# A two-layer GLA and SSD backbone in one program: one chunk's exponentials issued at another place, and a background computation paused over a layer norm

## The chip, the cores and the metric

The kernel runs on one core of a Trainium2 chip. The metric is the time of one execution on the device in microseconds (us); the time before is the median of three runs, 1932.36 us (1931.04 to 1933.9).

## What is computed

Two layers work on a stream of 512 latent tokens and 256 context tokens, 1024 channels each, all in float32. Layer 0 mixes tokens with gated linear attention (GLA, four heads), layer 1 with a bidirectional Mamba-2 state-space scan (SSD, eight groups of four heads of 64 channels, state of 128). Each mixer is followed by a squared-ReLU MLP of width 4096. Every sub-layer's input is modulated by a shift and a scale that come from the conditioning vectors, and its output by a gate; the sum with the residual goes through a layer norm.

```python
for i in range(DEPTH):                       # DEPTH = 2, kind 0 is GLA, kind 1 is SSD
    m_l = jnp.split((s_lat @ ada_w[i] + ada_b[i])[:, None, :], 6, axis=-1)
    ...
    hl = layer_norm(DEEPNORM_ALPHA * hl + m_l[2] * snake(yl), ln_g[i, 0], ln_b[i, 0])
    hl = layer_norm(DEEPNORM_ALPHA * hl + m_l[5] * sq_relu_mlp(modulate(hl, m_l[3], m_l[4]), ffn_w1[i], ffn_w2[i]), ...)

# SSD, one chunk of one direction; cum is the running sum of dt * a
seg = cum[:, :, None] - cum[:, None, :]
decay = jnp.exp(jnp.where(mask, seg, -jnp.inf))
cb = jnp.einsum('bign,bjgn->bijg', ci, bi)
y = jnp.einsum('bijg,bijgr,bjgrp->bigrp', cb, decay, xdt)
y = y + jnp.einsum('bign,bigr,bgrpn->bigrp', ci, jnp.exp(cum), s)
s_new = s * jnp.exp(last)[..., None, None] + jnp.einsum('bjgn,bjgr,bjgrp->bgrpn', bi, jnp.exp(last[:, None] - cum), xdt)
```

## The kernel before

**Products.** Channels lie on the 128 partitions and tokens along the free axis. Every weight matrix is read in blocks of 1024 x 128. A block is loaded by SP (`wload`, L258) and split in two parts that TensorE takes as fp32r: ScalarE (ACT) casts it to `wh` (L224) and VectorE (DVE) subtracts to get the rest `wl` (L225). `prod` (L265 to L273) then multiplies three times per block of 128 input channels: xh by wh, xl by wh, xh by wl, all at L271. These products, with 768, 512 or 384 token columns, are most of TensorE's (PE's) work.

**How side work is slotted in.** Each matmul in `prod` reports its columns to `worked` (L200 to L209). Every 768 columns are one unit. A list `side` holds Python generators with the inner work of the previous head or group, or with a layer norm; a generator that yields n is taken up again n units later. A second list, `background`, is advanced once in every `pace[0]` units, whenever the unit counter `clock[1]` is a multiple of it. `drain` runs the side generators to their end. So the place of inner work in the program is set by its yields, in units of matmul work. The framework's scheduler then orders the instructions of each engine by when it reckons their operands ready and by their place in the program; `tc.issue_after(ins)` keeps an instruction behind another one that it doesn't depend on.

**Background rows.** `ada_rows` (L154 to L182) computes the modulation vectors of later sub-layers on DVE: for each of eight blocks a load and one or two dot products over 1024 elements (L178), one block per step, each kept behind the last evacuation of the MLP (`behind`, L122). During the first MLP its items are the last rows of layer 0 and all of layer 1; the generator is appended at the end of the program's layer 0, where `pace[0]` is set to 21 (L1275).

**The first MLP's start.** `ffn` (L394) begins when the layer norm ahead of it is still under way. For the first two blocks of W1 it first multiplies the segments that are normalized (`presegs`, context and the first 256 latent tokens), then drains the layer norm, whose evacuation (L384 on ACT, L225 on DVE) brings the last 256 tokens, and then multiplies those (`restsegs`). After that `pace[0]` is 19, and from the second half of the first batch on 22.

**An SSD group.** `group(g)` (L938) projects and convolves the channels of group g: B, C, two blocks of x (`conv`: product, copy to `pre` on ACT at L914, five taps at L921 and L923, tanh form of SiLU at L925 and L926), then two gates. Then it appends `inner(g)`, which runs beside the products of group g + 1. Its steps, with the yields between them:

- At the start: eight row loads `ec` (L961) of cumulated decays, and for chunks 0 and 1 two tiles L each (L966), loaded by a broadcast row `crowc` (L968) and masked on GpSimd (POOL, L970). Ten L tiles exist.
- Transposition of B and x to natural layout (`natural`, L935, L936): `Bn`, `xnat`. Yields 1, 7, 7.
- States: products by decay weights (`prep`, `scaled_by`, L993), state contributions (`dS`, L1005), and the chain over chunks (`chain`, L993 and L1013). Yield 5, then the scores `cb` (L1025) and their copy `cbs` (L1027), yield 1, more of the chain, yield 2, the rest of it.
- For each half i of the head channels (`inter`): yield 4, an exponential of ec, four matmuls L1048 with the states, DVE products L1049, POOL sum L1050, DVE sum L1051 with the skip term.
- `decays` for a chunk: eight exponentials (L1060) over 128 x 128 on ACT, four for each direction, with the bias of their column. `ahead(c)` issues them behind the ACT instruction that `evac[0]` names, the last evacuation at that point. `ahead(0)` stands after `inter(0)`.
- For chunk c, every 14 units: `masks`, a POOL sum of both directions (L1063) and the DVE product with the scores (L1064), which is the mask tile; `ahead(c + 1)`; the rows of chunk c + 2; and in the next round `outputs` (four matmuls L1071 with xnat, two of 64 rows each side by side, and a DVE sum).

The functions that the change touches:

Of the kernel before, what the change touches and what calls it, by code (L numbers as in the profile page):

```python
# [12 lines left out]
AF = mybir.ActivationFunctionType  # L13
# [26 lines left out]
ZB = 2  # L40
# [23 lines left out]
def tile_backbone(ctx, tc, xT, cc, cr, vecs, rows, ada_w0, ada_wr, lnf, ffn_w1, ffn_w2,  # L64
                  gla_w_in, gla_w_v, gla_w_a, gla_a2, gla_w_out, ssd_w_in, ssd_w_dt, ssd_w_out, out):
    nc = tc.nc
# [18 lines left out]
    def nm(s):  # L85
        cnt[0] += 1
        return f"{s}_{cnt[0]}"
# [103 lines left out]
    clock = [0, 0]  # L191
# [19 lines left out]
    wait, pace = [0], [9]  # L211

    def drain(keep=0):
        while len(side) > keep:
            advance(side)
# [178 lines left out]
    def ffn(layer, xs, acc, segs, pool, npre, presegs, restsegs, passes, after):  # L394
# [29 lines left out]
        for bi, nb in enumerate((8, 8, 8, 8 - nlast, nlast)):  # L424
            ms = range(h0, h0 + nb)
            if bi == 0:
                drain(1)
                held = []
                for m in ms[:npre]:
                    held.append((weights(W1, m), mm_ps(segs)))  # L430
                    prod(held[-1][1], held[-1][0], xs, presegs, KT)
                drain()
                for m in ms[:npre]:
                    f1(m, restsegs, held[m])
                pace[0] = 19
                ms = ms[npre:]
            if bi == 4:
                ws = pair_weights(W2, h0, nb,
                                  lambda j: [pool.tile([P, NN], F32R, tag="rs", name=nm("ws"), bufs=20) for _ in range(2)])
            for m in ms:  # L440
                f1(m, segs if m == DFF // P - 1 else whole)
            ys = [rs[m] for m in range(h0, h0 + nb)]
            if bi == 0:
                gate = mod(layer, 5)
                pace[0] = 22
            if bi < 4:
                accum_proj(W2, h0, nb, ys, gate, acc, whole)
            else:
                accum_last(ws, ys, gate, acc, passes, after, early=None if layer == 0 else 5)
            h0 += nb  # L450
# [335 lines left out]
    def ssd_layer(xs, accd, acc0):  # L786
# [169 lines left out]
        def inner(g, fB, fC, fx, zs):  # L956
# [66 lines left out]
            for c in range(NLC):  # L1023
                cs = slice(c * P, (c + 1) * P)
                nc.tensor.matmul(cb[:, c, :], fB[:, cs], fC[:, cs], start=True, stop=True)  # L1025
            cbs = sp.tile([P, NLC, P], F32, tag="cbs", name=nm("cbs"), bufs=1)
            nc.scalar.copy(cbs, cb)  # L1027
            yield 1
            d03 = dS(*x03)
            chain(ST[1][:, 0], ST[0][:, 0], 0, 0, d03[:, 0])  # L1030
            chain(ST[2][:, 1], ST[3][:, 1], 3, 1, d03[:, 1])
# [18 lines left out]
                nc.gpsimd.tensor_add(T[:, i], T[:, i], E)  # L1050
                nc.vector.scalar_tensor_tensor(T[:, i], fx[i][:, 0:NL], dcol[:, 2 * g + i:2 * g + i + 1], T[:, i], ALU.mult, ALU.add)  # L1051

            def decays(c, L):
                for z, t in enumerate(L):
                    if z >= ZB:
                        nc.scalar.activation(t, t, AF.Exp)
                        continue
                    for h in range(4):
                        r = 32 * z + 4 * g + h
                        nc.scalar.activation(t[:, h, :], t[:, h, :], AF.Exp, bias=lcol[:, c, r:r + 1])  # L1060

            def masks(c, L):
                nc.gpsimd.tensor_add(L[0], L[0], L[1])  # L1063
                nc.vector.tensor_mul(L[0], L[0], cbs[:, c:c + 1, :].to_broadcast([P, 4, P]))  # L1064
# [8 lines left out]
                t = T[:, :, c * P:(c + 1) * P]  # L1073
                nc.vector.tensor_add(t, t, yp)

            def ahead(c):
                with tc.issue_after(evac[0].ins):
                    decays(c, Rs[c])

            for i in range(2):  # L1080
                yield SSDI[g == SG - 1]
                inter(i)
                if i == 0:
                    ahead(0)
            for c in range(NLC + 1):
                yield SSDY[g == SG - 1]
                if c > 0:
# [184 lines left out]
        return layer_norm(lnp, acc, sg[0][0], 256, nxt["ev"])  # L1272

    with phase("fp") as fp:
        pace[0] = 21  # L1275
        background.append(ada_rows([(0, 5)] + [(1, m) for m in range(6)],
                                   lambda s: fp.tile([P, D], F32, tag=f"srow{s}", name=f"srow{s}"),
                                   lambda: xn_tile("junk")))
        ffn(0, us, acc, BOTH, fp, 2, CTXL0, L1, (CTX, L0, L1), after0)
# [90 lines left out]
```

## Time and profile before

| | before |
|---|---|
| median of three runs | 1932.36 us |
| the profiled execution, whole | 1930.93 us |
| its span | 1929.2 us |
| mean granted TensorE clock | 0.994 |
| POOL sums L1063 | x32, mean 1499 ns |
| exponentials L1060 | x256, 80.5 us |
| weight casts L224 / subtractions L225 | x225, mean 1007 ns / x225, mean 1210 ns |

Engine shares stand in the prediction. A share is an average over the whole span, which has parts with different limits: GLA, then the first MLP (its first ReLU, L417, starts at 442.9 us), then SSD (its first ec load leaves SP at 1014.3 us, its last output matmul loads its weights at 1494.8 us), then the second MLP. The windows view divides the span and gives for each stretch the busy time of PE, PE's weight load (PEld), DVE, ACT and POOL, then granted clock, DMA share and GB/s. The timeline gives in each row start, duration, engine, line, operation, output and inputs, and in brackets how long the engine stood idle before it and whose end it waited for. Matmul ends are modelled. SPq is SP's DMA issuing.

### The profile page before, as it was taken

How to read it: one execution, taken by the hardware profiler on the slowest of the kernel's cores; microseconds unless marked ns; L12 is line 12 of the kernel's file. 1: busy time of each engine (PE TensorE's matmuls, PEld its weight loads, DVE VectorE, ACT ScalarE, POOL GpSimd, SP SyncE). 2: the span in 40 equal slices, each digit the busy share in tenths (PEclk: the TensorE clock that was granted, in tenths of full speed). 3: DMA queues.
4: the chain of work that ended last, by engine and by line, in shares of the span. 5: the costliest groups of instructions: out<-in, count | busy, mean ns of one | idle time of the engine just before them, and what ended most of it. 6: DMA issues, size and time to landing. Idle time of an engine off the chain costs nothing.

```text
span 1929.2 us, 28916 instructions
## 1 busy us (share of the span) xinstructions
PE 1865.5 (97%) x11365; PEld 1697.5 (88%) x11365; DVE 1270.7 (66%) x1972; ACT 797.4 (41%) x1410; POOL 402.7 (21%) x363
## 2 busy tenths in 40 slices
PE   7999999999999999999999999999999999999997
PEld 5988898899999999999998888888877888888886
DVE  4998867977665434444478898888896773333345
ACT  3445456456213112122266465555564352323231
POOL 2033231302102002010002443333331311102012
PEclk9999999999999999999999999999999999999999
DMA  9624203122444444423125444333443523333331
GB/s 356 192 64 144 77 26 99 33 97 88 153 136 127 134 129 142 131 79 103 55 79 142 137 132 125 105 118 112 126 124 117 158 72 96 95 99 99 96 91 54
DMA packets 79000, 219.08 MB, mean 114 GB/s; under 512 B 11088, under 2 KB 15824, under 8 KB 78864
## 3 DMA queue, kind: packets, MB, share of 16 engines
q1 hardware_dynamic: 78864, 217.24, 36.0%
q8 instruction: 89, 1.46, 0.3%
q14 instruction: 47, 0.39, 0.1%
HBM read 209.07 MB, written 8.13 MB: 113 GB/s over the span
## 4 chain that ended last, share of the span: by engine, by line
PE 64%; DVE 15%; issue 9%; ACT 4%; POOL 4%; DMA 3%; SPq 0%; DVEq 0%; POOLq 0%; ACTq 0%
PE mm L271 56%; DVE cv L923 3%; DMA L<-crowc 2%; DVE wl L225 1%; DVE A L629 1%; DVE E L640 1%; PE sm L712 1%; POOL ssum L1113 1%; PE mm L1218 1%; PE mm L556 1%; DVE cf L926 1%; POOL L L1063 1%; POOL T L1050 1%; PE sm L1218 1%; POOL W L648 1%
## 5 line engine op out<-in xcount | busy, mean ns | idle before, releaser
L271 PE MATMUL mm<-xh,wh 128*128 128x384 f32 (+2 forms) x1800 | 545.0, 356 | 1.4 <-ACT pre L914 0.9
L271 PE MATMUL mm<-xl,wh 128*128 128x384 f32 (+2 forms) x1800 | 541.1, 353 | 3.3 <-DVE xl L1119 3.2
L271 PE MATMUL mm<-xh,wl 128*128 128x384 f32 (+2 forms) x1800 | 539.6, 352 | 2.2 <-DVE wl L225 2.2
L224 ACT CAST wh<-raw 128x1024 fp32r<-128x1024 f32 (+3 forms) x225 | 226.3, 1007 | 669.8 <-PE mm L271 639.2
L225 DVE TENSOR_TENSOR wl<-raw,wh 128x1024 fp32r<-128x1024 f32 (+3 forms) x225 | 271.6, 1210 | 196.7 <-ACT wh L224 193.0
L271 PEld LDWEIGHTS mm<-xh,wh 128*128 128x128 f32 x1800 | 327.7, 189 | 30.7 <-issue 4.7
L271 PEld LDWEIGHTS mm<-xl,wh 128*128 128x128 f32 x1800 | 328.2, 189 | 29.8 <-DVE xl L1119 5.7
L271 PEld LDWEIGHTS mm<-xh,wl 128*128 128x128 f32 x1800 | 328.3, 189 | 27.4 <-DVE wl L225 3.2
L418 POOL TENSOR_TENSOR rq<-rr 128x768 f32<-128x768 f32 (+1 forms) x62 | 102.1, 1647 | 727.9 <-ACT rr L417 725.1
L454 DVE SCALAR_TENSOR_TENSOR acc<-mm,row,acc 128x256 f32<-128x256 f32 (+3 forms) x220 | 105.7, 517 | 205.9 <-PE mm L271 205.5
L271 PE MATMUL mm<-rl,wh 128*128 128x384 f32 (+1 forms) x704 | 211.2, 353 | 0.0
L271 PE MATMUL mm<-rh,wl 128*128 128x384 f32 (+1 forms) x704 | 211.1, 353 | 0.0
L271 PE MATMUL mm<-rh,wh 128*128 128x384 f32 (+1 forms) x704 | 211.1, 353 | 0.0
L923 DVE SCALAR_TENSOR_TENSOR cv<-pre,cvec,cv 128x770 f32<-128x770 f32 (+1 forms) x128 | 137.6, 1080 | 9.4 <-ACT cv L921 7.9
L271 PEld LDWEIGHTS mm<-rl,wh 128*128 128x128 f32 x704 | 128.9, 188 | 9.5
L271 PEld LDWEIGHTS mm<-rh,wh 128*128 128x128 f32 x704 | 128.8, 188 | 9.4
L271 PEld LDWEIGHTS mm<-rh,wl 128*128 128x128 f32 x704 | 128.9, 188 | 9.2
L420 DVE TENSOR_TENSOR rl<-rq,rh 128x768 fp32r<-128x768 f32 (+2 forms) x67 | 53.3, 795 | 76.2 <-POOL rq L418 75.9
L178 DVE SCALAR_TENSOR_TENSOR rawa<-rawa,srow 128x1024 f32<-128x1024 f32 x80 | 99.1, 1244 | 0.8
L970 POOL TENSOR_SCALAR_AFFINE_SELECT L<-L 128x512 f32<-128x512 f32 x64 | 62.7, 984 | 124.8 <-DMA L<-crowc 116.4
L1060 ACT ACTIVATE L<-L,lcol 128x128 f32<-128x128 f32 x256 | 80.5, 397 | 0.0
L1063 POOL TENSOR_TENSOR L<-L,L 128x512 f32<-128x512 f32 x32 | 48.0, 1499 | 147.7 <-ACT L L1060 147.7
(294 smaller groups left out, 2532.5 us busy)
## 6 DMA issues: line engine op xcount, KB each, us to landing
raw<-in_ffn_w_dram SPq DMA_DIRECT2D x112, 512.0 KB, 3.8
rawa<-in_ada_wr_dram SPq DMA_DIRECT2D x80, 512.0 KB, 3.6
raw<-in_ssd_w_in_dram SPq DMA_DIRECT2D x48, 512.0 KB, 3.6
L<-crowc SPq DMA_DIRECT2D x64, 256.0 KB, 3.7
raw<-in_ada_w_dram SPq DMA_DIRECT2D x16, 512.0 KB, 9.1
raw<-in_gla_w_in_dram SPq DMA_DIRECT2D x16, 512.0 KB, 4.5
ec<-crow SPq DMA_DIRECT2D x64, 128.0 KB, 2.9
acc<-in_xT_dram SPq DMA_DIRECT2D x14, 384.0 KB, 7.2
```

Of the source, the lines that this page charges most:

```text
L178: nc.vector.scalar_tensor_tensor(o, raw, 1.0, srow[s], ALU.mult, ALU.mult, accum_out=t[:, b, s:s + 1])
L224: nc.scalar.copy(h, src)
L225: nc.vector.tensor_sub(l, src, h.bitcast(F32))
L271: nc.tensor.matmul(part_of(ps, t0, n), a[:, k, :], b[:, t0:t0 + n], start=(k == 0 and i == 0), stop=(k == kt - 1 and i == 2))
L418: eng.tensor_mul(q[:, a:b], r[:, a:b], r[:, a:b])
L420: evacv[0] = nc.vector.tensor_sub(rl[:, a:b], q[:, a:b], rh[:, a:b].bitcast(F32))
L454: evacv[0] = nc.vector.scalar_tensor_tensor(acc[m][:, t0:t0 + n], part_of(ps, t0, n), gate[:, m, s:s + 1], (src or acc)[m][:, t0:t0 + n], ...
L923: nc.vector.scalar_tensor_tensor(c[:, 0:n], pre[:, t:t + n], cw(t), c[:, 0:n], ALU.mult, ALU.add)
L970: nc.gpsimd.affine_select(out=L[z], in_=L[z], compare_op=ALU.is_ge, fill=NEG, base=0, pattern=[[0, 4], [1 - 2 * z, P]], channel_multiplier ...
L1060: nc.scalar.activation(t[:, h, :], t[:, h, :], AF.Exp, bias=lcol[:, c, r:r + 1])
L1063: nc.gpsimd.tensor_add(L[0], L[0], L[1])
L1218: nc.tensor.matmul(part_of(first[j], t0, n), a[:, k, :], b[:, t0:t0 + n], start=(k == 0 and i == 0), stop=(k == KT - 1 and i == (1 if j == ...
```

## The change

```diff
--- before.py
+++ after.py
@@ -430,9 +430,10 @@
                     held.append((weights(W1, m), mm_ps(segs)))
                     prod(held[-1][1], held[-1][0], xs, presegs, KT)
                 drain()
+                clock[1] = 0
+                pace[0] = 17
                 for m in ms[:npre]:
                     f1(m, restsegs, held[m])
-                pace[0] = 19
                 ms = ms[npre:]
             if bi == 4:
                 ws = pair_weights(W2, h0, nb,
@@ -1024,8 +1025,22 @@
                 cs = slice(c * P, (c + 1) * P)
                 nc.tensor.matmul(cb[:, c, :], fB[:, cs], fC[:, cs], start=True, stop=True)
             cbs = sp.tile([P, NLC, P], F32, tag="cbs", name=nm("cbs"), bufs=1)
+            def decays(c, L):
+                for z, t in enumerate(L):
+                    if z >= ZB:
+                        nc.scalar.activation(t, t, AF.Exp)
+                        continue
+                    for h in range(4):
+                        r = 32 * z + 4 * g + h
+                        nc.scalar.activation(t[:, h, :], t[:, h, :], AF.Exp, bias=lcol[:, c, r:r + 1])
+
+            def ahead(c):
+                with tc.issue_after(evac[0].ins):
+                    decays(c, Rs[c])
+
             nc.scalar.copy(cbs, cb)
             yield 1
+            ahead(0)
             d03 = dS(*x03)
             chain(ST[1][:, 0], ST[0][:, 0], 0, 0, d03[:, 0])
             chain(ST[2][:, 1], ST[3][:, 1], 3, 1, d03[:, 1])
@@ -1050,15 +1065,6 @@
                 nc.gpsimd.tensor_add(T[:, i], T[:, i], E)
                 nc.vector.scalar_tensor_tensor(T[:, i], fx[i][:, 0:NL], dcol[:, 2 * g + i:2 * g + i + 1], T[:, i], ALU.mult, ALU.add)
 
-            def decays(c, L):
-                for z, t in enumerate(L):
-                    if z >= ZB:
-                        nc.scalar.activation(t, t, AF.Exp)
-                        continue
-                    for h in range(4):
-                        r = 32 * z + 4 * g + h
-                        nc.scalar.activation(t[:, h, :], t[:, h, :], AF.Exp, bias=lcol[:, c, r:r + 1])
-
             def masks(c, L):
                 nc.gpsimd.tensor_add(L[0], L[0], L[1])
                 nc.vector.tensor_mul(L[0], L[0], cbs[:, c:c + 1, :].to_broadcast([P, 4, P]))
@@ -1073,15 +1079,9 @@
                 t = T[:, :, c * P:(c + 1) * P]
                 nc.vector.tensor_add(t, t, yp)
 
-            def ahead(c):
-                with tc.issue_after(evac[0].ins):
-                    decays(c, Rs[c])
-
             for i in range(2):
                 yield SSDI[g == SG - 1]
                 inter(i)
-                if i == 0:
-                    ahead(0)
             for c in range(NLC + 1):
                 yield SSDY[g == SG - 1]
                 if c > 0:
@@ -1272,7 +1272,7 @@
         return layer_norm(lnp, acc, sg[0][0], 256, nxt["ev"])
 
     with phase("fp") as fp:
-        pace[0] = 21
+        pace[0] = 10 ** 9
         background.append(ada_rows([(0, 5)] + [(1, m) for m in range(6)],
                                    lambda s: fp.tile([P, D], F32, tag=f"srow{s}", name=f"srow{s}"),
                                    lambda: xn_tile("junk")))
```

**The exponentials.** `decays` and `ahead` are defined before the scores' copy, and `ahead(0)` stands right after that copy's `yield 1`. By the yields that is six units earlier in the program than before (2 and 4). At that point `evac[0]` is the last copy of `natural`, where it was the copy to `pre` of the next group's projection. No instruction is added or removed. The lines move: exponentials L1060 is now L1035, the copy cbs L1027 is L1041, L1048 to L1051 are L1063 to L1066, the POOL sum L1063 is L1069, the mask product L1064 is L1070, and the output matmul L1071 is L1077.

**The modulation rows.** `pace[0]` is set so high at the start of the first MLP that no background step falls into its beginning, and once the layer norm is drained the unit counter is set to 0 and the pace to 17. The 19 that followed the two `restsegs` products is gone; the 22 later stays.

The orders that follow are those of SSD group 1's inner work, beside the projections of group 2. In them `L_10338` and `L_10339` are the two directions' tiles of chunk 0, `L_10348` and `L_10349` those of chunk 1, `cbs` the scores, `pre`, `cv` and `cf` the convolution of the next group, `wh`, `wl` its weights, `T` the output sum, `ec` the row decays.

On ACT, from the last copy of xnat on, before:

```order
L936 COPY xnat_10359<-sm_10402 128x2x128
L1027 COPY cbs_10460<-sm_10455 128x512
L224 CAST wh_10705<-raw_10703 128x1024
L914 COPY pre_9493<-mm_10324 128x384
L914 COPY pre_9493<-mm_10325 128x128
L914 COPY pre_9493<-mm_10325 128x256
L1060 ACTIVATE L_10338<-L_10338,lcol 128x128
L921 ACTIVATE cv_10494<-pre_9493,cvec 128x770
L1060 ACTIVATE L_10338<-L_10338,lcol 128x128 x3
L1060 ACTIVATE L_10339<-L_10339,lcol 128x128 x4
L925 ACTIVATE cf_10495<-cv_10494 128x512
L925 ACTIVATE cf_10495<-cv_10494 128x256
```

And after:

```order
L937 COPY xnat_10359<-sm_10402 128x2x128
L1035 ACTIVATE L_10338<-L_10338,lcol 128x128 x4
L1035 ACTIVATE L_10339<-L_10339,lcol 128x128 x4
L1041 COPY cbs_10460<-sm_10455 128x512
L224 CAST wh_10705<-raw_10703 128x1024
L915 COPY pre_9493<-mm_10324 128x384
L915 COPY pre_9493<-mm_10325 128x128
L915 COPY pre_9493<-mm_10325 128x256
L922 ACTIVATE cv_10502<-pre_9493,cvec 128x770
L926 ACTIVATE cf_10503<-cv_10502 128x512
L926 ACTIVATE cf_10503<-cv_10502 128x256
L224 CAST wh_10800<-raw_10798 128x1024
```

The eight exponentials of chunk 0 stood behind the copies to `pre`; now they stand ahead of the copy of cbs. A weight cast now stands ahead of the next copy to `pre`.

On DVE, two stretches of group 1, the state chain and the place of the first mask product, before:

```order
L1013 TENSOR_TENSOR ST_10426<-ST_10426,sm_10481 128x256
L225 TENSOR_TENSOR wl_10706<-raw_10703,wh_10705 128x1024
L1013 TENSOR_TENSOR ST_10425<-ST_10425,sm_10483 128x256
L1051 SCALAR_TENSOR_TENSOR T_10493<-cf_10105,dcol,T_10493 128x512
L1049 TENSOR_TENSOR ec_10333<-sm_10557,ec_10333 128x512
L926 SCALAR_TENSOR_TENSOR cf_10495<-cf_10495,cv_10494 128x512
L926 SCALAR_TENSOR_TENSOR cf_10495<-cf_10495,cv_10494 128x256
L1051 SCALAR_TENSOR_TENSOR T_10493<-cf_10217,dcol,T_10493 128x512
L923 SCALAR_TENSOR_TENSOR cv_10577<-pre_9494,cvec,cv_10577 128x512
L1064 TENSOR_TENSOR L_10338<-L_10338,cbs_10460 128x512
L923 SCALAR_TENSOR_TENSOR cv_10577<-pre_9494,cvec,cv_10577 128x512 x2
L1064 TENSOR_TENSOR L_10348<-L_10348,cbs_10460 128x512
```

And after, the same two stretches:

```order
L1014 TENSOR_TENSOR ST_10426<-ST_10426,sm_10489 128x256
L1070 TENSOR_TENSOR L_10338<-L_10338,cbs_10460 128x512
L1014 TENSOR_TENSOR ST_10425<-ST_10425,sm_10491 128x256
L927 SCALAR_TENSOR_TENSOR cf_10503<-cf_10503,cv_10502 128x256
L1066 SCALAR_TENSOR_TENSOR T_10501<-cf_10217,dcol,T_10501 128x512
L225 TENSOR_TENSOR wl_10706<-raw_10703,wh_10705 128x1024
L924 SCALAR_TENSOR_TENSOR cv_10577<-pre_9494,cvec,cv_10577 128x512
L225 TENSOR_TENSOR wl_10801<-raw_10798,wh_10800 128x1024
L924 SCALAR_TENSOR_TENSOR cv_10577<-pre_9494,cvec,cv_10577 128x512
L1070 TENSOR_TENSOR L_10348<-L_10348,cbs_10460 128x512
```

The mask product of chunk 0 stands in the state chain, where the subtraction L225 of a weight block stood; that subtraction and the next block's stand behind the second half's sum L1066, and the product of chunk 1 behind them.

In groups 0 and 7 the order of no engine is changed. On SP the load of one weight block per group moves from before the eight `ec` loads of the next group to behind them.

## The prediction

> **What bounds the kernel now.** I read the page first: engine shares and the 40 slices.
>
> ```profile
> span 1929.2 us, 28916 instructions
> PE 1865.5 (97%) x11365; PEld 1697.5 (88%) x11365; DVE 1270.7 (66%) x1972; ACT 797.4 (41%) x1410; POOL 402.7 (21%) x363
> PE   7999999999999999999999999999999999999997
> DVE  4998867977665434444478898888896773333345
> ```
>
> The median of the three runs shown is 1932.36 us; the profiled execution took 1930.93 us, of which 1929.2 us are span, so 1.7 us lie around it. I work out the change against 1930.93 and put it on 1932.36. PE is busy for 97% of the span, so the kernel is bound by TensorE, and only what takes a wait of PE away, or adds one, changes the time. A busy PE does not yet mean that it gets its work in without pauses, so I next read the windows of 50 us, whose columns are length, then busy time and count for PE, PEld, DVE, ACT, POOL.
>
> ```profile
> 450.00:500.00 50.00, 50.00 (x300) 49.70 (x300) 34.40 (x50) 21.76 (x37) 12.99 (x7) 1.00 0.45 139
> 500.00:550.00 50.00, 50.00 (x291) 50.00 (x290) 32.52 (x55) 7.93 (x9) 1.74 (x1) 1.00 0.43 136
> 850.00:900.00 50.00, 50.00 (x290) 50.00 (x290) 17.24 (x28) 12.84 (x21) 6.15 (x4) 1.00 0.18 56
> 1150.00:1200.00 50.00, 48.03 (x282) 42.78 (x282) 44.60 (x64) 28.46 (x66) 18.71 (x15) 1.00 0.37 111
> ```
>
> In the first MLP (450 to 900 us) PE has no idle time at all. In the SSD layer (1000 to 1500 us) it has about 2 us in 50, and DVE is busy 44.6 us of 50. So I asked the view of waits what PE waits for from 1090 to 1440 us, where groups 1 to 6 of the SSD layer run; the columns are total us, times, longest.
>
> ```profile
> PE sm L1071 <- DMA ec<-crow: 7.9, 4, 2.0
> PE sm L1071 <- DVE L L1064: 4.1, 2, 2.1
> PE sm L935 <- ACT Bn L936: 0.7, 1, 0.7
> ```
>
> Six waits of about 2 us, one in each group, all at L1071, the multiplication of a chunk's decayed scores with xnat: that is nearly all that PE loses there. The rest of the reading is the timeline of one such group (start, us, engine, line), which gives the chain behind the wait.
>
> ```profile
> 1098.92 1.64 ACT L936 COPY xnat<-sm 128x512 f32<-128x512 f32 x4
> 1106.51 0.59 ACT L1027 COPY cbs<-sm 128x512 f32<-128x512 f32 x1 [5.94 <-PE sm L1025]
> 1109.86 0.42 ACT L1060 ACTIVATE L<-L,lcol 128x128 f32<-128x128 f32 x1
> 1111.09 2.15 ACT L1060 ACTIVATE L<-L,lcol 128x128 f32<-128x128 f32 x7
> 1113.31 1.41 POOL L1063 TENSOR_TENSOR L<-L,L 128x512 f32<-128x512 f32 x1 [12.60 <-ACT L L1060]
> 1118.22 0.87 POOL L970 TENSOR_SCALAR_AFFINE_SELECT L<-L 128x512 f32<-128x512 f32 x1 [3.50 <-DMA L<-crowc]
> 1119.07 1.29 POOL L1050 TENSOR_TENSOR T<-T,ec 128x512 f32<-128x512 f32 x1
> 1125.53 1.74 POOL L1063 TENSOR_TENSOR L<-L,L 128x512 f32<-128x512 f32 x1 [0.59 <-ACT L L1060]
> 1104.76 0.43 DVE L993 TENSOR_TENSOR ST<-sm,dtot 128x256 f32<-128x256 f32 x1 [2.06 <-PE sm L1005]
> 1109.76 1.23 DVE L225 TENSOR_TENSOR wl<-raw,wh 128x1024 fp32r<-128x1024 f32 x1
> 1120.40 0.75 DVE L1051 SCALAR_TENSOR_TENSOR T<-cf,dcol,T 128x512 f32<-128x512 f32 x1 [1.80 <-POOL T L1050]
> 1126.08 1.75 DVE L1064 TENSOR_TENSOR L<-L,cbs 128x512 f32<-128x512 f32 x1
> 1129.19 0.68 DVE L1064 TENSOR_TENSOR L<-L,cbs 128x512 f32<-128x512 f32 x1
> 1128.08 0.66 PE L1071 MATMUL sm<-L,xnat 128*64 128x128 f32 x8 [1.95 <-DMA ec<-crow]
> 1133.75 0.66 PE L1071 MATMUL sm<-L,xnat 128*64 128x128 f32 x8
> ```
>
> PE's wait ends at 1128.08, 0.25 us after the mask multiplication L1064 ends (1126.08 + 1.75 = 1127.83); the DMA that the view names there is not an operand of L1071. The POOL sum L1063 that L1064 needs had ended at 1114.72, so L1064 was not late for its operand: it is late because it stands far back in DVE's queue, behind L1051 work that itself waits 1.80 us for POOL. POOL in turn sat 3.50 us in front of L970, which needs a row load of the next group that could start only when L1063 had freed its buffer.
>
> **The exponentials, part by part.** No instruction is added or removed; eight exponentials (L1060) per group stand earlier. ACT is idle for 5.94 us before 1106.51, from 1100.56 on (1098.92 + 1.64). By the row at 1111.09 seven take 2.15 us, so eight take about 2.5 us: they would run from 1100.6 to 1103.1, inside that gap, and the copy cbs that follows still waits for PE until 1106.51. Their cost is therefore nothing; it would be 2.5 us of ACT per group if the gap were gone. Their tiles are a group's first rows, loaded and masked before the previous group ended, so I see no new wait in front of them.
>
> L1063 follows at about 1103.2 instead of 1113.31, and ends at 1104.6, when DVE is waiting for PE anyway (2.06 us before 1104.76). DVE's new order has the mask multiplication after a state update near 1109.7, where the weight subtraction L225 stood; its operands (L1063, cbs) are there by 1107.1, so it costs its 0.68 us (row at 1129.19, alone) in place of 1.23. It ends some 15 us before PE wants it. So the wait at L1071 goes wholly.
>
> What is late next? The second L1071 stood at 1133.75 and would come at 1131.6. Its mask multiplication ended at 1129.87, and must not slip past 1131.6. Two subtractions L225 (1.23 each) now stand ahead of it, one from the state chain and one from after it. Against them DVE wins 0.68 + 0.07 us in the state chain (first L225 out, first L1064 in: 1.23 against 0.68, with the rest from the 2.06 us gap), 1.80 us of waiting at L1051, since POOL's L970 gets its row load at 1104.6 instead of 1114.74 and no longer blocks L1050 at 1119.07, and the 1.75 us of the first L1064. That is about 4 us won against 2.5 us of L225 and at most 1.05 us for the next row.
>
> ```profile
> 1119.48 0.57 ACT L914 COPY pre<-mm 128x512 f32<-128x512 f32 x1
> 1125.35 1.04 ACT L224 CAST wh<-raw 128x1024 fp32r<-128x1024 f32 x1
> 1132.06 0.90 ACT L914 COPY pre<-mm 128x384 f32<-128x384 f32 x3
> 1146.34 1.05 ACT L224 CAST wh<-raw 128x1024 fp32r<-128x1024 f32 x1 [1.99 <-PE mm L271]
> 1111.01 0.33 SPq L258 DMA_DIRECT2D raw<-in_ssd_w_in_dram  x1
> 1120.39 5.51 SPq L961 DMA_DIRECT2D ec<-crow  x8
> ```
>
> The weight cast L224 of 1.04 us at 1125.35 now stands ahead of the evacuation at 1119.48, so what is queued behind it on ACT (the copy, L921, the second chunk's exponentials) comes up to 1.05 us later; PE's next two banks are free without that copy, and the next product runs until 1132.06. I take nothing for PE. On SP the weight load of 1111.01 now stands behind the eight row loads ec, whose last ones wait for the second L1050; it would leave SP near 1124 to 1126, and its cast is the one at 1146.34. A cover of 20 us: nothing. The second ec exponential moves ahead of the copy at 1132.06, which would now come near 1130; its loads left SP by 1125.9 even in the old order (1120.39 + 5.51). Nothing again, with one microsecond of margin at the worst.
>
> So six waits go. The rows of the waits view add up to 7.9 + 4.1 = 12.0 us of idle time. That counts from a matmul's modelled end; the pace of a fed PE is 50.00/291 = 0.17 us per matmul while each is shown as 0.35 us long (row below), so the loss is 0.18 us more each, 13.1 us in all. Between the two I take 12.5.
>
> ```profile
> L271 PE MATMUL mm<-xl,wh 128*128 128x384 f32 (+2 forms) x1800 | 541.1, 353 | 3.3 <-DVE xl L1119 3.2
> ```
>
> One rule speaks against the move. The row at 1126.08 shows L1064 at 1.75 us beside POOL's L1063 (1125.53 to 1127.27); the one at 1129.19 took 0.68. The Trainium skill ("SBUF — State Buffer", section "Who interferes with whom") says that a VectorE instruction with two SBUF inputs and a GpSimd instruction that reads SBUF block each other for the whole instruction; the trace agrees, since 1127.27 + 0.56 is where L1064 ends. L1063 and L970 now move beside the state chain at 1102 to 1109, whose multiplications by dtot read SBUF twice. L1063 falls into DVE's 2.06 us gap; L970, 0.87 us, can hold a step of the chain up for that long, less the 0.55 us that the swap of L225 for L1064 gives it. If PE's L1048 waited for the remaining 0.32 us in each group, 1.9 us would be lost; I count half a microsecond in the choice of 12.5 over 13.1 and let the range hold the rest.
>
> **The modulation rows.** The two products L178 that stood among the first MLP's layer norm move behind it.
>
> ```profile
> 446.99 1.22 DVE L178 SCALAR_TENSOR_TENSOR junk<-rawa,srow 128x1024 f32<-128x1024 f32 x1
> 449.71 1.22 DVE L178 SCALAR_TENSOR_TENSOR rawa<-rawa,srow 128x1024 f32<-128x1024 f32 x1
> 454.92 0.42 DVE L225 TENSOR_TENSOR xl<-lnu,xh 128x256 fp32r<-128x256 f32 x1
> 449.50 1.02 ACT L384 ACTIVATE lnu<-sm,l00B,l00G 128x256 f32<-128x256 f32 x2 [1.10 <-DVE acc L386]
> 452.22 1.02 ACT L384 ACTIVATE lnu<-sm,l00B,l00G 128x256 f32<-128x256 f32 x2 [1.10 <-DVE acc L386]
> ```
>
> They take 2.44 us of DVE and make ACT wait 1.10 us twice; without them the last split of the layer norm, at 454.92, ends near 452.8. But PE is fully busy from 450 us on: it fills that time with the next product's matmuls, which in the new order come after the short ones. So the gain is nothing, and the cost is nothing as long as the splits come those 2.5 us earlier. If they did not, PE would want the last one near 453.4 and get it at 455.34: at most 1.9 us lost. The L178 that were held are caught up within four weight blocks; DVE is busy 34.40 us of 50 there and PE waits for none of it. I take 0, with 0 to 1.9 us of cost as bounds; a gain is excluded, since PE has no idle time there to win.
>
> The sum: 1930.93 - 12.5 + 0 = 1918.4 for a profiled execution, and 1932.36 - 12.5 = 1919.9 for the median.
>
> **The rivals.** *The next mask takes its place (0.13).* If DVE, busy 44.6 of 50 us, does not keep the 4 us that I count as won, the second L1071 waits instead. Each microsecond that its L1064 ends after 1131.6 costs 6 us over the six groups; with one, 1932.36 - 12.5 + 6 = 1925.9. For it: DVE shows no idle time to speak of after 1126. Against it: the margin of 1.7 us before anything is won.
>
> *Small losses (0.10).* The SBUF collision of above (1.9 us) or the order in the MLP (1.9 us): 1921.8 with either.
>
> *Nothing (0.05).* The waits view names a load of ec for four of the six waits. Were L1071 really held by that, it would stay, and the time with it: 1932.4. Against it: the same 0.25 us after L1064 in all of them.
>
> *Slower (0.04).* The cast that stands ahead of the evacuation at 1119.48 holds up the fC convolution, DVE runs out of work there and then has two L225 to do ahead of the second mask. From the point where that L1064 ends later than 1133.75 (PE's old place, 3.9 us after its old end) the group is longer than before; with one microsecond more, 1932.36 + 6 = 1938.4. Against it: the bound above is 3.5 us of new work in front, even if nothing were won.
>
> **How the numbers follow.** The forecast, 1919.9, gets 0.68, the rivals the chances named. Its own bounds are 13.1 us and 12.0 us won, with runs 1.4 us to either side of their median: 1917.5 to 1922. The small losses lie in this, the next mask reaches to 1926, and nothing and slower (0.09) are left out with the far half of the next mask: 1917 to 1926.5. A difference of 0.2% (3.9 us) is about what a measurement of this kernel can tell from none. Faster than 1928.5: 0.68 + 0.10 + most of 0.13 = 0.90; within 0.2%: 0.06; slower: 0.04.
>
> **What would show it.** Right: in the waits from 1085 to 1430 us no L1071 with 2 us; eight exponentials in a row before cbs; the first POOL sum of a group (L1063 in the old numbering) some 10 us earlier within the group, L1051 without its 1.8 us; groups 2 us shorter each; the windows from 450 to 900 us still at 50.00. Wrong in the first term: waits of PE at the second L1071, at L1048 or at a transposition L935 that add up to more than 2 us. Wrong in the second: idle time of PE between 446 and 460 us. Wrong altogether: a kernel whose L1071 waits stay, or whose windows of the SSD layer show DVE at 50 of 50 us.

## The result, and the profile after

The changed kernel took 1919.06 us (median of 5 runs, 1915.99 to 1919.53) against 1932.36 us before (median of 5, 1931.04 to 1933.9). The ratio, taken over all runs here and below and so not quite the quotient of the medians, is 0.9928, with a 95% interval of 0.9916 to 0.9939: 0.7% faster. The forecast was 1919.9 us. The profiled execution took 1919.44 us, 1917.7 us of it span, 11.5 us less than the profiled one of before.

The page of the changed kernel, its span and the engines' busy time:

```profile
span 1917.7 us, 28913 instructions
PE 1867.2 (97%) x11365; PEld 1698.3 (89%) x11365; DVE 1268.2 (66%) x1972; ACT 796.4 (42%) x1410; POOL 400.5 (21%) x363
```

And its windows of 50 us, with the columns that the prediction names:

```profile
450.00:500.00 50.00, 50.00 (x298) 49.71 (x297) 33.65 (x49) 19.63 (x32) 13.13 (x7) 1.00 0.45 141
1150.00:1200.00 50.00, 50.00 (x295) 43.88 (x294) 46.60 (x69) 30.51 (x70) 17.74 (x14) 1.00 0.39 123
1200.00:1250.00 50.00, 50.00 (x291) 44.39 (x290) 44.17 (x67) 28.01 (x65) 18.44 (x15) 1.00 0.40 121
```

In the SSD layer PE is busy for 50.00 of 50 us where it was busy for about 48; the first MLP had 50.00 before and has 50.00 now. The waits of PE from 1085 to 1430 us, where the six of 2 us each stood at the output matmul (L1071, now L1077), now hold only these two rows:

```profile
PE mm L271 <- ACT xh L1118: 0.8, 1, 0.8
PE sm L936 <- ACT Bn L937: 0.6, 1, 0.6
```

The timeline of group 1 answers to the one that the prediction shows (start, us, engine, line):

```profile
1099.98 2.49 ACT L1035 ACTIVATE L<-L,lcol 128x128 f32<-128x128 f32 x8
1106.08 0.59 ACT L1041 COPY cbs<-sm 128x512 f32<-128x512 f32 x1 [3.61 <-PE sm L1026]
...
1102.55 1.29 POOL L1069 TENSOR_TENSOR L<-L,L 128x512 f32<-128x512 f32 x1 [2.26 <-ACT L L1035]
1107.03 0.88 POOL L971 TENSOR_SCALAR_AFFINE_SELECT L<-L 128x512 f32<-128x512 f32 x1 [3.20 <-DMA L<-crowc]
1114.84 1.99 POOL L1065 TENSOR_TENSOR T<-T,ec 128x512 f32<-128x512 f32 x1 [6.92 <-DVE ec L1064]
1124.08 1.32 POOL L1069 TENSOR_TENSOR L<-L,L 128x512 f32<-128x512 f32 x1 [2.58 <-ACT L L1035]
...
1104.33 0.42 DVE L994 TENSOR_TENSOR ST<-sm,dtot 128x256 f32<-128x256 f32 x1 [2.05 <-PE sm L1006]
1109.34 0.69 DVE L1070 TENSOR_TENSOR L<-L,cbs 128x512 f32<-128x512 f32 x1
1116.86 0.75 DVE L1066 SCALAR_TENSOR_TENSOR T<-cf,dcol,T 128x512 f32<-128x512 f32 x1 [1.18 <-POOL T L1065]
1124.17 2.31 DVE L225 TENSOR_TENSOR wl<-raw,wh 128x1024 fp32r<-128x1024 f32 x1
1128.18 0.68 DVE L1070 TENSOR_TENSOR L<-L,cbs 128x512 f32<-128x512 f32 x1
...
1125.67 0.66 PE L1077 MATMUL sm<-L,xnat 128*64 128x128 f32 x8
1131.32 0.66 PE L1077 MATMUL sm<-L,xnat 128*64 128x128 f32 x8
```

The eight exponentials stand in ACT's gap ahead of the scores' copy, which still waits for PE. The POOL sum (L1069) falls into DVE's wait before 1104.33, and the mask product (L1070) ends at 1110.03, 15.6 us before PE wants it at 1125.67. The second output matmul comes at 1131.32, and its mask product ends at 1128.86, 2.5 us before.

What a group is worth is read from the starts of the first output matmul in neighbouring groups, here in before and then in after:

```profile
1300.55 0.66 PE L1071 MATMUL sm<-L,xnat 128*64 128x128 f32 x8 [1.97 <-DMA ec<-crow]
1357.97 0.66 PE L1071 MATMUL sm<-L,xnat 128*64 128x128 f32 x8 [1.97 <-DMA ec<-crow]
1416.94 0.66 PE L1071 MATMUL sm<-L,xnat 128*64 128x128 f32 x8 [1.97 <-DMA ec<-crow]
```

```profile
1181.22 0.66 PE L1077 MATMUL sm<-L,xnat 128*64 128x128 f32 x8
1236.63 0.66 PE L1077 MATMUL sm<-L,xnat 128*64 128x128 f32 x8
```

After, this group takes 55.41 us (groups 1 to 5 take 55.41 to 55.80). Before, one took 57.42 us (1300.55 to 1357.97), 2.01 more, and the next one 58.97, 3.56 more, with the same wait. The windows of 5 us of before around the waits that end at 1300.55 and 1357.97 say why; the column after the five engines is the granted clock:

```profile
1298.00:1303.00 5.00, 3.03 (x23) 2.57 (x22) 4.96 (x6) 0.83 (x1) 2.62 (x2) 1.00 0.67 196
1303.00:1308.00 5.00, 5.00 (x34) 4.58 (x34) 4.11 (x6) 4.58 (x11) 2.33 (x2) 1.00 0.31 74
1355.00:1360.00 5.00, 3.03 (x18) 2.56 (x17) 4.96 (x7) 1.26 (x3) 1.94 (x2) 0.85 0.65 167
1360.00:1365.00 5.00, 5.00 (x25) 4.92 (x24) 4.43 (x6) 4.54 (x11) 2.67 (x3) 0.81 0.70 104
```

Behind the first the clock stayed at 1.00; behind the second it fell (0.85 and 0.81 in these windows), and the group lost another 1.5 us. This the prediction had not seen. When a wait does this is read from the traces at the end.

### The profile page after: what moved, and what is told of

It reads as the page before. It is cut to its first block, busy times and chain, and to the rows that moved or that the text cites. A ratio compares the mean times of both kernels' runs of the same rounds, so it can differ in the third digit from the quotient of the medians.

```text
span 1917.7 us, 28913 instructions
## 1 busy us (share of the span) xinstructions
PE 1867.2 (97%) x11365; PEld 1698.3 (89%) x11365; DVE 1268.2 (66%) x1972; ACT 796.4 (42%) x1410; POOL 400.5 (21%) x363
## 4 chain that ended last, share of the span: by engine, by line
PE 78%; DVE 13%; ACT 4%; issue 3%; POOL 1%; DMA 1%; SPq 0%; DVEq 0%; ACTq 0%; POOLq 0%
PE mm L271 66%; DVE cv L924 1%; PE sm L1063 1%; DVE A L630 1%; PE sm L713 1%; DVE E L641 1%; PE sm L1006 1%; PE mm L1218 1%; PE mm L557 1%; DVE wl L225 1%; PE sm L1077 1%; PE sm L682 1%; PE sm L936 1%; PE sm L1218 1%; POOL W L649 1%
## 5 line engine op out<-in xcount | busy, mean ns | idle before, releaser
L225 DVE TENSOR_TENSOR wl<-raw,wh 128x1024 fp32r<-128x1024 f32 (+3 forms) x225 | 276.8, 1234 | 195.5 <-ACT wh L224 191.8
L178 DVE SCALAR_TENSOR_TENSOR rawa<-rawa,srow 128x1024 f32<-128x1024 f32 x80 | 97.9, 1230 | 0.7
L926 ACT ACTIVATE cf<-cv 128x512 f32<-128x512 f32 (+1 forms) x56 | 27.5, 534 | 137.1 <-DVE cv L924 137.1
L971 POOL TENSOR_SCALAR_AFFINE_SELECT L<-L 128x512 f32<-128x512 f32 x64 | 59.6, 934 | 117.8 <-DMA L<-crowc 113.1
L1035 ACT ACTIVATE L<-L,lcol 128x128 f32<-128x128 f32 x256 | 79.8, 398 | 0.0
```

The costliest lines, as they stand in the source:

```text
L178: nc.vector.scalar_tensor_tensor(o, raw, 1.0, srow[s], ALU.mult, ALU.mult, accum_out=t[:, b, s:s + 1])
L225: nc.vector.tensor_sub(l, src, h.bitcast(F32))
L926: nc.scalar.activation(f[:, t0:t1], c[:, t0 + d:t1 + d], AF.Tanh)
L971: nc.gpsimd.affine_select(out=L[z], in_=L[z], compare_op=ALU.is_ge, fill=NEG, base=0, pattern=[[0, 4], [1 - 2 * z, P]], channel_multiplier ...
```

## The experiments

The theory: PE waited for the mask product of chunk 0, which came late on DVE. Two things made it late: its place in DVE's queue behind the skip sums (L1051), and POOL, on which these sums waited, since POOL sat in front of L970, whose row load could start only when the late POOL sum had freed its buffer. The change moves the product ahead of these sums and POOL's wait to an earlier time. Rivals: the modulation rows carry part of the gain; the exponentials' ACT time does; the ec loads that the waits view names do.

**The two parts apart.** e1 takes the change without its first and last hunk; e2 takes only these:

```diff
-        pace[0] = 21
+        pace[0] = 10 ** 9
...
                 drain()
+                clock[1] = 0
+                pace[0] = 17
                 for m in ms[:npre]:
                     f1(m, restsegs, held[m])
-                pace[0] = 19
```

e1 was expected so:

> The exponentials moved as in the change, the modulation rows left as before. My theory (all of the gain is the six waits at the output matmul; the rows are worth nothing): 1919 to 1920 us, and no wait of 2 us at that matmul. Rival (the rows carry part of the 13.3 us by which the medians differ, which is more than the 12.0 us of the waits view): 1921 to 1922 us.

e2:

> The modulation rows held and paced as in the change, the exponentials where they were. My theory: no difference, 1931.5 to 1933 us, the six waits of 2.1 us all there, PE busy 50 of 50 us from 450 us on. Rival (the rows carry part): 1930 to 1931 us.

e1 took 1918.75 us (before beside it 1932.53; ratio 0.9937, interval 0.9924 to 0.9949) and e2 1931.01 us (0.9993, 0.9984 to 1.0002). All of the gain that can be measured is the exponentials'. The median of e2 lies below the range that I expected and at the edge of the rival's. Its interval holds no change, and it does not exclude that the rows are worth up to 3 us; its profile shows nothing of it. PE is as busy from 450 us on as before, and the six waits are there:

```profile
PE sm L1072 <- DMA ec<-crow: 7.8, 4, 2.0
PE sm L1072 <- DVE L L1065: 4.0, 2, 2.1
```

**Early exponentials, late product.** e3 starts from the changed kernel and puts the mask product back to where it stood in DVE's queue:

```diff
+                tsum[0] = nc.vector.scalar_tensor_tensor(T[:, i], fx[i][:, 0:NL], ...)
...
                 nc.gpsimd.tensor_add(L[0], L[0], L[1])
+                with tc.issue_after(tsum[0].ins):
+                    nc.vector.tensor_mul(L[0], L[0], cbs[:, c:c + 1, :].to_broadcast([P, 4, P]))
```

> After, but with the mask product on DVE held behind the second half's sum with the skip term, so that it stands where it stood before; exponentials and the POOL sum stay early. Theory U (the early exponentials count because the early POOL sum frees a buffer, so that POOL is not held by a row load and the sums that the product stands behind come earlier): the product ends near 1124 in group 1, PE wants it at 1125.7, no wait, 1919 to 1921 us. Theory Q (the product's place in DVE's queue decides): the waits of 2.1 us come back, 1931 to 1933 us. Between them, waits of 0.5 to 1 us, 1923 to 1926 us, would say that both have a share.

It took 1921.8 us (0.9955, 0.9941 to 0.9968). In groups 1 to 6 no wait came back, though the product stood where it had stood; in group 0, where the hold applies as well, a new one of 1.7 us did (e9, which holds the product in the same way, has it too: 1.66 us). The output matmul of group 0, then the product and the matmul of group 1:

```profile
1072.35 0.66 PE L1080 MATMUL sm<-L,xnat 128*64 128x128 f32 x8 [1.67 <-issue]
...
1123.67 0.68 DVE L1073 TENSOR_TENSOR L<-L,cbs 128x512 f32<-128x512 f32 x1
...
1125.73 0.66 PE L1080 MATMUL sm<-L,xnat 128*64 128x128 f32 x8
```

The product ends at 1124.35, 1.4 us before the matmul: the early exponentials and their POOL sum are enough without the product's new place, as theory U had it. It is not quite as good, and the time lies just above theory U's range: the wait in group 0 is 1.7 us, and most groups take 55.8 us against 55.4.

**Late exponentials, early product.** e4 starts from before:

```diff
                 if i == 0:
                     ahead(0)
+                    Ms[0] = masks(0, Rs.pop(0))
...
-                if c < NLC:
+                if 0 < c < NLC:
                     Ms[c] = masks(c, Rs.pop(c))
```

> Before, but the POOL sum and the mask product of chunk 0 are issued right behind its exponentials, at the old place of these; rows as before. On DVE the product stands ahead of both sums with the skip term. Theory Q: it ends near 1118.5, PE wants it near 1126, the waits go, 1919 to 1921 us. Theory U alone: POOL is held by the row load as before, the second half's sums stay late, but the product no longer stands behind them, so the first wait goes as well; a wait of up to 1 us at the second output matmul would show that the late sums still cost, 1921 to 1926 us. Rival E (the exponentials take ACT time that the next convolution needs, and that is what the change gave back): no gain, 1931 to 1933 us.

It took 1917.56 us (0.9929, 0.9917 to 0.9942), as much of a gain as the change itself and a little more than I expected, with every exponential at its old place. The product ends at 1117.39, and the skip sum behind it still waits 1.81 us for POOL, now at no cost:

```profile
1116.71 0.68 DVE L1064 TENSOR_TENSOR L<-L,cbs 128x512 f32<-128x512 f32 x1
1120.13 0.76 DVE L1051 SCALAR_TENSOR_TENSOR T<-cf,dcol,T 128x512 f32<-128x512 f32 x1 [1.81 <-POOL T L1050]
...
1125.79 0.66 PE L1071 MATMUL sm<-L,xnat 128*64 128x128 f32 x8
```

So either cure takes the six waits away alone. That rules out ACT's time as what was won, and the ec loads too: in e4 group 1's eight leave SP from 1120.12 on, as before (1120.39), and PE doesn't wait.

**POOL alone.** e5 starts from before and moves nothing but the masking of the next group's row tile on POOL:

```diff
+                    with tc.issue_after(psum[0].ins) if c == 1 and psum[0] else nullcontext():
+                        nc.gpsimd.affine_select(out=L[z], in_=L[z], compare_op=ALU.is_ge, fill=NEG, base=0, ...)
...
-                nc.gpsimd.tensor_add(T[:, i], T[:, i], E)
+                psum[0] = nc.gpsimd.tensor_add(T[:, i], T[:, i], E)
```

> Before, with one POOL instruction per group moved: the masking of the next group's row tile, on which POOL sat 3.5 us, now stands behind both sums of the halves. Exponentials, POOL sum of the masks, the mask product's place in DVE's queue and the modulation rows stay as before. Theory U (DVE's product was late because the skip sums ahead of it waited for POOL): the sum of the first half comes about 1.2 to 1.8 us earlier on POOL, the product ends 1.5 to 2.5 us earlier, the waits fall from 2.1 to between 0 and 0.6 us, 1919 to 1923 us. Theory Q (only its place behind those sums counts, not POOL): the waits stay near 2.1 us, 1931 to 1933 us.

It took 1921.06 us (before beside it 1931.53; 0.995, 0.9937 to 0.9964). The waits fall from about 2 us to 0.7 in the view, a little more than the 0 to 0.6 that I expected to be left. What is left has a cause that the timeline shows:

```profile
1116.91 0.75 DVE L1052 SCALAR_TENSOR_TENSOR T<-cf,dcol,T 128x512 f32<-128x512 f32 x1 [1.18 <-POOL T L1051]
1123.46 1.77 DVE L1065 TENSOR_TENSOR L<-L,cbs 128x512 f32<-128x512 f32 x1
...
1123.19 1.49 POOL L1064 TENSOR_TENSOR L<-L,L 128x512 f32<-128x512 f32 x1 [0.86 <-ACT L L1061]
...
1125.49 0.66 PE L1072 MATMUL sm<-L,xnat 128*64 128x128 f32 x8 [0.69 <-ACT L L1061]
```

The product starts at 1123.46, early enough, and takes 1.77 us beside the POOL sum that began at 1123.19; at the 0.68 us that it takes alone (the row at 1128.18 above) it would end at 1124.14, and PE wanted it at 1124.8 (1125.49 less 0.69). The view names the exponentials here, which had been done for a while. So POOL's hold was about two thirds of the old wait. That the rest is the meeting with the POOL sum follows from these rows; no run takes that meeting away alone.

**What covers the exponentials.** e6 and e7 add 8 and 16 exponentials that nobody uses behind chunk 0's in all groups, e11 16 in groups 1 to 6 only, and e10 is the changed kernel beside e11:

```diff
             ahead(0)
+            with tc.issue_after(evac[0].ins):
+                for _ in range(16):
+                    nc.scalar.activation(jk, ident, AF.Exp)
```

e6:

> After, with eight more exponentials of 128 x 128 into a tile that nobody reads, right behind chunk 0's, in every group. In the profile of after ACT is idle for 3.61 us ahead of the scores' copy of group 1; eight take about 2.5 us. If that cover is real, nothing changes: 1918 to 1920 us. If ACT time in this stage costs what it takes, 2.5 us in eight groups, 1935 to 1939 us.

e7:

> After, with sixteen more such exponentials per group, 4.9 us, of which two stand behind the scores' copy. The cover of 3.61 us is used up: the scores' copy comes 0.7 to 1.3 us later. Theory: behind the copy ACT had another idle microsecond, and the mask product has 15 us to spare, so still close to nothing, 1918 to 1922 us. If the cover's end shows at once: 0.7 to 1.3 us in each of six to eight groups, 1923 to 1930 us.

e10:

> The changed kernel as it is, on the chip of the next run, as its yardstick: 1917 to 1920 us. If the kernels with more exponentials were faster (1914.7 and 1915.8 us) only because of the chip or the clock that was granted, it comes out at 1915 to 1917 us here.

e11:

> After, with sixteen more exponentials in groups 1 to 6 only; the orders in groups 0 and 7 stay those of after. If more work on ACT in the groups 1 to 6 is really for nothing: within 1.5 us of the run of after beside it. If it makes the kernel faster: 3 to 4 us below. If what made the other two faster lies in the changed order of group 7: equal to after here.

They took 1915.77 us (0.9921, 0.9908 to 0.9934), 1914.73 (0.9914, 0.99 to 0.9927), 1919.52 (0.9936, 0.9922 to 0.9949) and 1918.11 (0.9927, 0.9914 to 0.994). The cover is real, and more of ACT is free than the gap of 3.61 us. ACT in group 1 of e7:

```profile
1098.02 2.48 ACT L1035 ACTIVATE L<-L,lcol 128x128 f32<-128x128 f32 x8
1100.38 4.77 ACT L1047 ACTIVATE jk<-ident 128x128 f32<-128x128 f32 x14
1105.05 0.57 ACT L1041 COPY cbs<-sm 128x512 f32<-128x512 f32 x1
```

Fourteen of the sixteen stand ahead of the copy of the scores, which follows without a pause. It ends 18.1 us before the first output matmul (1123.71 in e7), against 19.0 in the changed kernel, and PE waits for nothing behind it. That e6 and e7 came out 3 to 4 us below the changed kernel was not expected; e11, with the same load as e7 in groups 1 to 6, is within 1.5 us of e10. That points to groups 0 and 7, but doesn't show it: e6 and e7 ran on another chip than e10 and e11. In the traces the last group, from the first output matmul of group 6 to that of group 7, is 61.7 to 62.0 us in e6 and e7 and 63.1 to 63.8 in e1, e10, e11 and the changed kernel. That is 1 to 2 of the 3 to 4 us. Why is open; the intervals overlap, so that even the difference is not certain.

**The rows at their worst.** e8 is before with one number changed:

```diff
-        pace[0] = 21
+        pace[0] = 4
```

> Before, with the background pace 4 in place of 21 at the start of the first MLP: six modulation products stand among the first MLP's layer norm instead of two, 4.9 us more of DVE there, and the rest of the rows comes sooner. Theory (PE has other products to fill that time with, so even this costs nothing): 1931 to 1934 us, PE busy 50 of 50 us from 450 us on. If the layer norm's tail sets PE's pace: 2 to 5 us more, 1934 to 1937 us, with idle time of PE between 450 and 470 us.

It took 1955.82 us (1.0125, 1.0111 to 1.0139), and neither theory had that. Not the layer norm's tail is hit: PE waits once, for a weight subtraction.

```profile
PE mm L271 <- DVE wl L225: 20.4, 1, 20.4
```

Behind the layer norm DVE had 18 of the products L178 queued ahead of that subtraction, and worked through them from 457.4 to 484.5 us:

```profile
457.44 1.21 DVE L178 SCALAR_TENSOR_TENSOR junk<-rawa,srow 128x1024 f32<-128x1024 f32 x1
484.54 1.21 DVE L225 TENSOR_TENSOR wl<-raw,wh 128x1024 fp32r<-128x1024 f32 x1
...
485.81 1.01 PE L271 MATMUL mm<-xh,wl 128*128 128x384 f32 x2 [20.39 <-DVE wl L225]
```

**A longer wait.** e9 is before with two copies on DVE that nobody uses, between the second skip sum and the mask product, in groups 1 to 6 (the hold behind that sum applies in all groups):

```diff
+                late = tsum[0]
+                if c == 0 and 0 < g < SG - 1:
+                    for j in range(2):
+                        with tc.issue_after(late.ins):
+                            late = nc.vector.tensor_copy(jk, xn[:, 0])
+                with tc.issue_after(late.ins):
+                    nc.vector.tensor_mul(L[0], L[0], cbs[:, c:c + 1, :].to_broadcast([P, 4, P]))
```

> Before, with two DVE copies of 128 x 256 into a tile that nobody reads, between the second half's sum and chunk 0's mask product in groups 1 to 6. With the convolution steps that come between, the product starts some 2 us later and the wait at the output matmul grows from 2.1 to about 4 us. If a wait costs only its idle time: 12 to 13 us more, 1943 to 1946 us. If a wait also lowers the granted clock behind it (in the runs so far it fell for about 8 us, worth some 1.5 us, behind one to three of the six waits of 2.1 us, and behind none of 0.85 us): the longer waits do it more often, the groups take 1.5 us more than their idle time says, and the time is 1946 to 1952 us.

It took 1952.06 us (before beside it 1931.57; 1.0104, 1.009 to 1.0118), at the upper edge of what I expected if a wait also costs clock. The waits view gives the sum of the waits:

```profile
PE sm L1080 <- DVE L L1073: 22.1, 6, 3.7
```

The timeline shows the first output matmul of two neighbouring groups:

```profile
1315.51 1.12 PE L1080 MATMUL sm<-L,xnat 128*64 128x128 f32 x8 [3.70 <-DVE L L1073]
1376.98 1.12 PE L1080 MATMUL sm<-L,xnat 128*64 128x128 f32 x8 [3.67 <-DVE L L1073]
```

And in the windows of 5 us behind two of the waits the granted clock is 0.50:

```profile
1130.00:1135.00 5.00, 4.47 (x19) 4.17 (x20) 4.87 (x7) 3.30 (x6) 1.86 (x2) 0.50 0.50 100
1191.00:1196.00 5.00, 3.62 (x16) 3.32 (x17) 4.91 (x8) 2.52 (x3) 2.22 (x2) 0.50 0.47 127
```

A group takes 61.47 us, 6.06 more than the 55.41 of after, for a wait of 3.7 us in the view. The clock falls to half at each of the six, for 6.8 us, of which 5.1 to 5.8 us lie behind the wait; that goes with the other 2.4 us. PE waits 10.1 us more than before in the view (22.1 less 12.0) and 1.7 us in group 0, and the kernel is 20.5 us slower.

| run | us | before beside it | PE's wait at chunk 0's output matmul, groups 1 to 6 |
|---|---|---|---|
| the change | 1919.06 | 1932.36 | none |
| e1, exponentials only | 1918.75 | 1932.53 | none |
| e2, rows only | 1931.01 | 1932.53 | 2 us each |
| e3, early exponentials, late product | 1921.8 | 1932.53 | none (1.7 us in group 0) |
| e4, late exponentials, early product | 1917.56 | 1932.53 | none |
| e5, POOL not held | 1921.06 | 1931.53 | 0.7 us each |
| e6, eight more | 1915.77 | 1931.53 | none |
| e7, sixteen more | 1914.73 | 1931.53 | none |
| e8, pace 4 | 1955.82 | 1931.53 | 2 us each |
| e9, longer wait | 1952.06 | 1931.57 | 3.7 us each (1.7 us in group 0) |
| e10, the change again | 1919.52 | 1931.57 | none |
| e11, sixteen more, groups 1 to 6 | 1918.11 | 1931.57 | none |

## Why the prediction was right

*The first term*, six waits gone, held with its mechanism. The waits are gone from the view; e4 shows that the product's lateness was the cause, e5 that POOL's wait for the row load made most of it, and e3 that the product is in time behind the skip sums once the POOL sum is early. The rival on the ec loads falls with e4: there the loads stay and the waits go.

*Its size*, 12.5 us, came out so near partly by luck. From the first output matmul of group 0 to that of group 6 it is 345.15 us before (1071.79 to 1416.94) and 331.82 after (1071.43 to 1403.25), 13.3 less: five steps of 1.6 to 2.2 us, and one of 3.56, where the clock's fall went with the wait. The 0.18 us per wait that I added for the modelled ends does not show: a group with a wait of 1.97 us and no fall took 2.01 more. And 1.9 us were given back in the last group: from there to group 7's first output matmul it is 61.63 us before and 63.50 after. The fall and what was given back, neither of which I had foreseen, nearly cancel in these two executions. Where the output projection begins, PE waits for the first splits of y, and in after the clock falls there:

```profile
1427.93 0.51 PE L271 MATMUL mm<-xh,wh 128*128 128x512 f32 x1 [0.78 <-ACT xh L1118]
1430.35 0.80 PE L271 MATMUL mm<-xl,wh 128*128 128x512 f32 x1 [1.92 <-DVE xl L1119]
```

The window of 5 us in which the second wait ends:

```profile
1430.00:1435.00 5.00, 4.65 (x17) 4.09 (x18) 5.00 (x6) 3.77 (x8) 1.44 (x1) 0.50 0.42 135
```

Before, three waits of 0.6 to 1.2 us stood there and the clock stayed up. In e10 it stayed up as well, and the group was 63.2 us long; its waits add up to 6.0 us against 4.2 before (without the one that ends at 1416.94), which covers the 1.5 us that it is longer. Why the splits come later for PE in the changed order is open. The profiled executions differ by 11.5 us, the medians of the changed kernel and its before by 13.3 and 12.0 (e10), and of e4 and its before by 15.0; the forecast of 12.5 lies among them.

*The steps.* The exponentials ran from 1099.98 to 1102.47 (I had 1100.6 to 1103.1), at no cost, as said; e7 puts 4.8 us more in front of the copy. The mask product took 0.69 us in the state chain. The wait of the skip sum for POOL did not go, as I had said it would: it fell from 1.80 to 1.18 us, since POOL's own sum (L1065) of 1.7 to 2 us remains. So 0.6 us less was won in front of the second mask than I had counted, and its margin is 2.5 us; it had 3.9 before (1129.87 and 1133.75). The next mask did come closer to taking the place, and did not. L971 beside the state chain cost nothing (0.88 us at 1107.03, the steps of DVE beside it as long as before, no wait of PE behind it). The collision went elsewhere: the second L225 takes 2.31 us at 1124.17 beside L1069, and it too had room.

*The modulation rows*, 0, held (e2). But the bound of 1.9 us of harm was taken from the wrong place. I looked at the layer norm's splits; e8 shows that what the rows can hold up is the weight subtraction behind them, and that this costs 24 us when enough of them pile up.

## What to carry to other kernels

When PE waits for an operand, follow the producer back through its engine's queue until an instruction with a wait of its own appears; here that was a POOL instruction in front of a row load, three steps away from the matmul, and moving that one instruction was worth 10 of the 13 us. A late step in a chain can have two cures of which either is enough (an earlier operand, an earlier place in the queue), and they don't add up. Work that fills an engine "in the background" is priced by what stands behind it in that engine's queue, not by the stage in which it was placed.

## What the runs showed of the hardware

A wait of PE can cost more than its length. Counted over the six groups of each profiled run, the granted clock fell at none of the six waits of 0.7 us (e5), at 7 of 18 of 2 us (1 in before, 3 in e2, 3 in e8), and at all six of 3.7 us (e9), each time to half: for 3.4 us at the waits of 2 us (not the 8 of e9's expectation) and for 6.8 us at the longer ones. A fall cost 1.5 to 1.7 us at the waits of 2 us and 2.3 to 2.7 us at the longer ones, by the length of the groups. In no profiled run without these waits did the clock fall between 1085 and 1420 us.

Which wait it is can be read from the traces. Within a run the granted clock changes only at points that lie whole multiples of 3.413 us apart: the first and the last of e9's six falls begin at 1129.54 and 1436.74, 90 times 3.413 us. Cut by this grid, two of the waits of before look so (length, then PE's busy time; the clock stands behind the five engines):

```profile
1297.06:1300.47 3.41, 1.52 (x9) 1.20 (x7) 3.41 (x4) 1.77 (x4) 2.12 (x2) 1.00 0.60 181
1300.47:1303.88 3.41, 3.33 (x24) 3.19 (x25) 3.38 (x5) 0.46 (x1) 1.36 (x2) 1.00 0.61 189
1355.08:1358.49 3.41, 1.44 (x14) 1.05 (x12) 3.38 (x5) 1.18 (x2) 1.77 (x1) 1.00 0.61 192
1358.49:1361.90 3.41, 3.41 (x13) 3.34 (x11) 3.41 (x6) 1.44 (x2) 1.10 (x1) 0.50 0.93 109
```

The first wait is cut in two, 1.89 us of it in one stretch, and the clock stays; the second lies whole in one stretch, 1.97 us, and the clock is half in the next. The 7 waits of 18 that lie whole in a stretch are the 7 with a fall. In all 13 profiled runs, from 1060 to 1490 us, the clock fell behind every stretch with 1.92 us or more of idle time and behind none with 1.89 or less. So it looks like chance only because the grid lies differently in each execution; no run was made to test the bound. In e9 the next stretch holds another 1.0 to 1.7 us of the wait, and the clock stays at half for one stretch more.

The Trainium skill ("TensorE: Matmul & The Clock Gate", section "What's actually happening") says that the array goes to half its clock after an idle window of about 3.4 us and comes back after as long a busy one, and that the window runs freely. The 0.50 agrees with the half, the falls of 3.4 us with the time to come back, and the grid with a window that runs freely. The length does not agree as a limit: 1.92 us of idle time within 3.41 were enough here.

Where a DVE product of two SBUF operands met a POOL sum, the one that started second took longer. In e5 the POOL sum began 0.27 us before the product, which took 1.77 us in place of 0.68; in e3 the product began 0.10 us before the sum and took 0.68, and the sum took 1.73 in place of 1.27.
